# Modulation of the second block: both transfers of a step issued first, then its four one-column products, those of the later transfer leading

## The chip, the cores and the metric

The kernel runs on one core of a Trainium2 chip. A core has a matrix engine (TensorE, PE in the profile), three engines for elementwise work (VectorE, DVE; ScalarE, ACT; GpSimd, POOL), an engine that mostly issues transfers (SyncE, SP) and 16 DMA engines between main memory and the core's on-chip memory. The metric is the device time of one execution in microseconds (us), the median over several runs.

## The reference

Two transformer-like blocks on a sequence of 1024-wide vectors. The first has two layers, each with a pair of recurrent mixers, cross-attention to a memory and a convolutional feed-forward part. The second is conditioned on a vector `c`: six vectors of 1024 numbers each are made from it and shift, scale and gate the block's hybrid mixer (dilated attention beside a gated recurrence) and its mixture of 32 experts.

```python
def second_block(x, c, w_ada, b_ada, ...):
    cond = jax.nn.silu(c)
    mod = cond @ w_ada[l] + b_ada[l]        # 1024 x 6144
    ...                                     # shift, scale, gate of the mixer; shift, scale, gate of the experts
```

The change touches only how `cond @ w_ada` is fed and ordered.

## The kernel before, in words

**The modulation.** `Net.ada` (L1458) computes `mod` as 6144 = 3 x 2048 numbers. Round r of three covers 2048 columns, which stand as four rows of 512 in one bank of the matrix engine's result memory, at partitions 0, 32, 64 and 96. A round has eight steps, k = 0 to 7, one for each 128 of the 1024 input rows. A step brings 128 x 2048 numbers of `w_ada` as two transfers of 128 x 1024 (512 KB each, L1478) into two `raw` tiles, and adds four products to the bank: the stationary operand is one column, `cond[:, k]`, the moving one 128 x 512 of the tile, and the result one row, j = 0 to 3. Rows j = 0, 1 come from the first tile, j = 2, 3 from the second. Each product goes through the helper `mm` (L362), which is why all matrix products of the profile show that line, and each shows as two records. After the last step of a round VectorE adds the bias to the four rows (L1485).

**Where the steps run.** `ada` is a generator. The program calls `fill(point)` at named points of the other work, and a table gives how many steps are drawn there: 18 steps in the RWKV mixer of the first layer (l16, l32, r2, r3, r4), two at xn1 and three at xc1 (around the second layer's cross-attention). The last step is drawn by `drain("a")` at L1695, in the second block's mixer, ahead of `mod_rest` (L1512). `mod_rest` turns the rows into columns (products mc, L1496), makes the gate `gate_m` (products bc, copies L1521) and prepares the router (products rb, `brow` at L265).

**Buffers.** The `raw` tiles come from a pool of five that the modulation shares with the loader of the other weights (`wunit`, L365 on), so a transfer waits on SP until the products that read that buffer are done.

**Order.** The kernel is written with pools and tiles, and a scheduler orders the instructions of each engine when the program is built (L2530). Code that is written in another order can thus shift other instructions too, also far from the place. Names in rows: `mk`, `px`, `pxt`, `py`, `pak`, `pz`, `pm`, `pu` are products of the RWKV mixer; `sc`, `pt`, `po` the score, transpose and output products of the cross-attention (HPT is the copy of pt, L1095); `tm`, `pj` projections, `pa`, `pk`, `pd` the gated recurrence and `as`, `apt`, `pv` the attention of the second block's mixer (HaS its scores, L1720 to L1725, HaPT the copy of apt); `gu`, `dn`, `dx` products of the experts.

Of the kernel before, what the change touches and what calls it, by code (L numbers as in the profile page):

```python
# [225 lines left out]
class Net:  # L226
# [1232 lines left out]
    def ada(self, mrow):  # L1459

        nc = self.nc
        W = self.dr["w_ada_2"][0]
        cond, th = self.cp.tile([128, 8], F32, name="cond"), self.cp.tile([128, 8], F32, name="cth")
        nc.scalar.activation(th, self.V("c"), AF.Tanh, scale=0.5)
        nc.vector.scalar_tensor_tensor(cond, th, 1.0, self.V("c"), op0=OP.add, op1=OP.mult)
        nc.vector.tensor_scalar(cond, cond, 0.5, None, op0=OP.mult)
        for r in range(3):
            nc.sync.dma_start(mrow[r][0:128:32, :], self.dr["b_ada_2"][0, 2048 * r:2048 * r + 2048].rearrange("(j c) -> j c", j=4))
        for u, name in enumerate(("g_post_mix_2", "g_post_ffn_2")):
            nc.sync.dma_start(mrow[3][64 * u:64 * u + 64:32, :], self.dr[name][0].rearrange("(j c) -> j c", j=2))  # L1470
        for r in range(3):
            ps = self.ps("ada")
            for k in range(8):
                for u in range(2):
                    self.n += 1
                    raw = self.rawp.tile([128, 1024], F32, tag="raw", name=f"raw_{self.n}")
                    c0 = 2048 * r + 1024 * u
                    nc.sync.dma_start(raw, W[128 * k:128 * k + 128, c0:c0 + 1024])  # L1478
                    for v in range(2):
                        j = 2 * u + v  # L1480
                        self.mm(ps[32 * j:32 * j + 1, :], cond[:, k:k + 1], raw[:, 512 * v:512 * v + 512], start=(k == 0), stop=(k == 7))
                if k == 7:
                    for j in range(4):
                        row = mrow[r][32 * j:32 * j + 1, :]
                        nc.vector.tensor_tensor(row, ps[32 * j:32 * j + 1, :], row, op=OP.add)  # L1485
                self.nada += 1
                yield 1
# [1046 lines left out]
```

## Time and profile before

| what | us |
|---|---|
| median of 3 runs (2145.54 to 2147.9) | 2145.57 |
| the profiled execution | 2153.04 |
| its span, first to last instruction | 2150.9 |

The trace is of one execution on the chip. PE, DVE, ACT, POOL and SP are the engines; PEld is the load of a stationary operand, which goes on beside products. A row of the timeline gives the start, the duration, the instruction and, in brackets, how long the engine had been idle and what ended that. The granted clock (PEclk) is the share of full speed that TensorE was given. The mean granted clock of the whole span is 0.966.

### The profile page before, as it was taken

Reading aid. Unit: us, or ns where it says so; the run is one execution under the profiler, and the core shown is the slowest. Engines: PE = TensorE matmul, PEld = TensorE weight load, DVE = VectorE, ACT = ScalarE, POOL = GpSimd, SP = SyncE. Lnnn points to the kernel's source line nnn. Section 1 sums busy time; section 2 is a strip of 40 time slices with the busy share of each in tenths; the row PEclk is TensorE's granted clock in tenths of the full one; section 3 lists DMA queues with packets and bytes.
Section 4 is the critical chain, followed back from the end, with each engine's and each line's share of the span. In section 5 each row is a group of like instructions: output and inputs, shape, how many; then the busy total and the mean of one; then the engine's idle time right before and its main releaser. Section 6 shows DMA issues by size and latency. Waiting matters only on the chain.

```text
span 2150.9 us, 37883 instructions
## 1 busy us (share of the span) xinstructions
PE 2015.1 (94%) x15056; PEld 1286.3 (60%) x15056; DVE 937.9 (44%) x1854; ACT 670.9 (31%) x1331; POOL 74.7 (3%) x97
## 2 busy tenths in 40 slices
PE   7999999999997899998989999999999999999997
PEld 6876798999985789997874333333233333333332
DVE  6764655777766457778554111111141111111122
ACT  6523554555654355555333100000000100000011
POOL 1200000000000000002001000000000000000000
PEclk9999999999998899999989999999999999999999
DMA  7459454666634546665858999999899999999992
GB/s 210 147 190 289 126 171 128 192 190 181 184 108 118 166 137 187 182 187 159 310 193 298 376 412 412 412 412 412 359 354 409 409 410 409 410 411 411 407 386 91
DMA packets 327765, 589.14 MB, mean 274 GB/s; under 512 B 25778, under 2 KB 216626, under 8 KB 318242
## 3 DMA queue, kind: packets, MB, share of 16 engines
q1 hardware_dynamic: 327586, 586.70, 76.7%
q8 instruction: 119, 1.95, 0.4%
q14 instruction: 60, 0.49, 0.1%
HBM read 585.58 MB, written 1.05 MB: 273 GB/s over the span
## 4 chain that ended last, share of the span: by engine, by line
PE 87%; DVE 4%; ACT 2%; issue 1%; DMA 1%; POOL 1%; ACTq 0%; SPq 0%; DVEq 0%; POOLq 0%
PE gu L362 22%; PE dn L362 13%; PE ug L362 11%; PE acc L362 9%; PE pj L362 6%; PE mk L362 4%; PE cb L362 3%; PE dx L362 3%; PE qp L362 2%; PE ada L362 1%; PE po L362 1%; PE tm L362 1%; PE accd L362 1%; PE at L2209 1%; DMA raw<-in_w_ada_dram 1%
## 5 line engine op out<-in xcount | busy, mean ns | idle before, releaser
L388 DVE TENSOR_TENSOR lo<-raw,hi 128x512 fp32r<-128x512 f32 x578 | 378.7, 695 | 162.2 <-ACT hi L387 146.8
L387 ACT CAST hi<-raw 128x512 fp32r<-128x512 f32 x578 | 328.7, 618 | 325.4 <-issue 85.0
L362 PE MATMUL gu<-Bring,xg 128*32 128x512 f32 (+1 forms) x3000 | 373.0, 594 | 0.0
L362 PEld LDWEIGHTS gu<-Bring,xg 128*32 128x32 f32 (+1 forms) x3000 | 110.9, 111 | 239.1 <-issue 219.3
L362 PE MATMUL dn<-Bring,ya 128*32 128x512 f32 (+2 forms) x1688 | 231.3, 599 | 1.3
L2317 DVE TENSOR_SCALAR sg<-gu 128x512 f32<-128x512 f32 x32 | 20.6, 686 | 433.1 <-PE gu L362 433.1
L362 PE MATMUL ug<-Bxh,hi 128*128 128x256 f32 x688 | 193.9, 282 | 1.4 <-ACT Bxh L487 1.4
L362 PE MATMUL ug<-Bxl,hi 128*128 128x256 f32 x688 | 193.7, 282 | 0.3 <-DVE Bxl L488 0.3
L362 PE MATMUL ug<-Bxh,lo 128*128 128x256 f32 x688 | 193.6, 282 | 0.0
L2318 ACT ACTIVATE sg<-sg 128x512 f32<-128x512 f32 x32 | 19.7, 629 | 506.6 <-DVE sg L2317 506.6
L362 PE MATMUL gu<-ring,xg 128*32 128x512 f32 (+1 forms) x968 | 174.2, 596 | 0.0
L362 PE MATMUL pj<-Bxh,hi 128*128 128x256 f32 x472 | 140.4, 298 | 8.6 <-ACT hi L387 4.1
L362 PE MATMUL pj<-Bxh,lo 128*128 128x256 f32 x472 | 138.0, 294 | 2.4 <-DVE lo L388 2.4
L362 PE MATMUL pj<-Bxl,hi 128*128 128x256 f32 x472 | 137.4, 292 | 0.9 <-DVE Bxl L488 0.6
L362 PEld LDWEIGHTS dn<-Bring,ya 128*32 128x32 f32 (+1 forms) x1688 | 60.7, 113 | 125.7 <-issue 112.5
L362 PEld LDWEIGHTS ug<-Bxh,hi 128*128 128x128 f32 x688 | 129.8, 189 | 3.9 <-ACT Bxh L487 1.8
L362 PEld LDWEIGHTS ug<-Bxl,hi 128*128 128x128 f32 x688 | 130.2, 189 | 1.9 <-DVE Bxl L488 0.5
L362 PEld LDWEIGHTS ug<-Bxh,lo 128*128 128x128 f32 x688 | 130.1, 189 | 0.0
L362 PEld LDWEIGHTS pj<-Bxh,hi 128*128 128x128 f32 x472 | 93.0, 197 | 13.5 <-ACT hi L387 5.3
L362 PEld LDWEIGHTS pj<-Bxh,lo 128*128 128x128 f32 x472 | 92.5, 196 | 5.2 <-DVE lo L388 3.0
L362 PEld LDWEIGHTS pj<-Bxl,hi 128*128 128x128 f32 x472 | 92.9, 197 | 3.8 <-issue 1.8
L362 PEld LDWEIGHTS gu<-ring,xg 128*32 128x32 f32 (+1 forms) x968 | 47.3, 111 | 75.9 <-issue 73.4
(725 smaller groups left out, 3141.5 us busy)
## 6 DMA issues: line engine op xcount, KB each, us to landing
Bring<-in_w_gu_dram SPq DMA_DIRECT2D x366, 512.0 KB, 10.2
Bring<-in_w_down_dram SPq DMA_DIRECT2D x198, 512.0 KB, 10.8
ring<-in_w_gu_dram SPq DMA_DIRECT2D x73, 1024.0 KB, 12.5
raw<-in_ffn_w_up_dram SPq DMA_DIRECT2D x84, 512.0 KB, 4.2
ring<-in_w_down_dram SPq DMA_DIRECT2D x29, 1024.0 KB, 13.3
raw<-in_w_ada_dram SPq DMA_DIRECT2D x48, 512.0 KB, 5.0
raw<-in_ffn_w_down_dram SPq DMA_DIRECT2D x42, 512.0 KB, 3.6
raw<-in_xattn_wkv_dram SPq DMA_DIRECT2D x32, 512.0 KB, 4.0
```

Of the source, the lines that this page charges most:

```text
L362: return self.nc.tensor.matmul(out, lhsT, rhs, start=start, stop=stop, skip_group_check=True)
L387: nc.scalar.copy(hi[:, s], raw[:, s])
L388: nc.vector.tensor_tensor(lo[:, s], raw[:, s], hi[:, s].bitcast(F32), op=OP.subtract)
L2209: nc.tensor.transpose(pt[:, f, :], act[:, 128 * f:128 * f + 128], self.ident)
L2317: nc.vector.tensor_scalar(g, pglu, 7.0, None, op0=OP.min)
L2318: nc.scalar.activation(g, g, AF.Silu, scale=1.702)
```

## The change

In `ada` a step now asks for both tiles and issues both transfers first, and then runs its four products in the order j = 2, 3, 0, 1, so that the two fed by the second transfer come first.

```diff
             for k in range(8):
+                raws = []
                 for u in range(2):
                     self.n += 1
                     raw = self.rawp.tile([128, 1024], F32, tag="raw", name=f"raw_{self.n}")
                     c0 = 2048 * r + 1024 * u
                     nc.sync.dma_start(raw, W[128 * k:128 * k + 128, c0:c0 + 1024])
-                    for v in range(2):
-                        j = 2 * u + v
-                        self.mm(ps[32 * j:32 * j + 1, :], cond[:, k:k + 1], raw[:, 512 * v:512 * v + 512], start=(k == 0), stop=(k == 7))
+                    raws.append(raw)
+
+                for j in (2, 3, 0, 1):
+                    self.mm(ps[32 * j:32 * j + 1, :], cond[:, k:k + 1], raws[j // 2][:, 512 * (j % 2):512 * (j % 2) + 512], start=(k == 0), stop=(k == 7))
                 if k == 7:
```

On TensorE, at the three steps drawn at xc1 in the cross-attention of the second layer (`ada_2117` is the bank, `raw_...` the tile a pair of products reads; lines with - are of the kernel before, with + of the changed one):

```order
 L362 MATMUL sc_7816<-BkT_221,Bq_7529 128x256 x4
+L362 MATMUL ada_2117<-raw_7919,cond 1x512 x2
 L362 MATMUL ada_2117<-raw_7917,cond 1x512 x2
-L362 MATMUL ada_2117<-raw_7921,cond 1x512 x2
+L362 MATMUL ada_2117<-raw_7927,cond 1x512 x2
 L362 MATMUL ada_2117<-raw_7925,cond 1x512 x2
-L362 MATMUL ada_2117<-raw_7929,cond 1x512 x2
+L1093 MATMUL pt_7831<-c_70,BP_7799 128x128
+L362 MATMUL ada_2117<-raw_7935,cond 1x512 x2
 L362 MATMUL ada_2117<-raw_7933,cond 1x512 x2
-L1093 MATMUL pt_7831<-c_70,BP_7799 128x128
 L1093 MATMUL pt_7831<-c_70,BP_7800 128x128
```

The second tile of each step (7919, 7927, 7935 now; 7921, 7929, 7937 before) leads, and the last step stands as a group of four behind the first transpose pt. Before, five pairs ran ahead of the four transposes and one behind them.

On TensorE, at the end of the last step, in the second block's mixer: before, both pairs stand further up among the tm products, and behind the last pk there comes

```order
L1667 MATMUL pk_10750<-c_70,Bkd_10517 128x128
L1496 MATMUL mc_10910<-c_70,Bmrow_225 128x128 x4
L1496 MATMUL mc_10916<-c_70,Bmrow_226 128x128 x4
L362 MATMUL bc_10923<-Bmrow_225,c_70 128x512
L362 MATMUL bc_10926<-Bmrow_225,c_70 128x512
L362 MATMUL pd_10765<-Hvx_10763,Hkt_10752 128x512
L362 MATMUL rb_10934<-wr,modc 1x32 x8
```

and in the changed kernel, at the same place,

```order
L1669 MATMUL pk_10750<-c_70,Bkd_10517 128x128
L362 MATMUL ada_2117<-raw_10895,cond 1x512
L1498 MATMUL mc_10910<-c_70,Bmrow_225 128x128 x4
L362 MATMUL pd_10765<-Hvx_10763,Hkt_10752 128x512
L362 MATMUL pd_10773<-Hvx_10771,Hkt_10752 128x512
L362 MATMUL pd_10781<-Hvx_10779,Hkt_10752 128x512
L362 MATMUL pd_10789<-Hvx_10787,Hkt_10752 128x512
L1498 MATMUL mc_10916<-c_70,Bmrow_226 128x128 x4
L362 MATMUL bc_10923<-Bmrow_225,c_70 128x512
L362 MATMUL bc_10926<-Bmrow_225,c_70 128x512
L362 MATMUL rb_10934<-wr,modc 1x32 x8
```

The last product of the modulation has moved behind the last pk; the transposes mc of row block 226 and what follows them stand behind four pd products instead of ahead of them.

On TensorE, in the attention of the same mixer, behind the last of the tm products (one piece of the difference):

```order
 L362 MATMUL tm_11216<-lo_11280,Bxh_10312 128x512
-L362 MATMUL as_11333<-Bka_10949,Bqa_10948 128x128 x2
-L362 MATMUL as_11357<-Bka_10949,Bqa_10948 128x256
-L1729 MATMUL apt_11322<-c_70,HaS_11316 128x128 x4
-L362 MATMUL as_11357<-Bka_10949,Bqa_10948 128x256
+L362 MATMUL as_11313<-Bka_10949,Bqa_10948 128x256 x2
+L362 MATMUL as_11333<-Bka_10949,Bqa_10948 128x128 x4
+L362 MATMUL as_11357<-Bka_10949,Bqa_10948 128x256 x2
 L362 MATMUL as_11377<-Bka_10949,Bqa_10948 128x256 x2
 L362 MATMUL as_11397<-Bka_10949,Bqa_10948 128x128 x4
+L1731 MATMUL apt_11322<-c_70,HaS_11316 128x128 x4
```

The first score products (as_11313 and half of as_11333) stood 24 tm products earlier; they now stand behind the last of them, a few products ahead of the transposes apt_11322 that read their result.

## Rows read from the trace of the kernel before

**Rows 1.** The page: chain that ended last, shares by engine.
```profile
PE 87%; DVE 4%; ACT 2%; issue 1%; DMA 1%; POOL 1%; ACTq 0%; SPq 0%; DVEq 0%; POOLq 0%
```
**Rows 2.** Windows: length, busy (instructions) of each engine, PEclk, DMA share, GB/s.
```profile
150.00:200.00 50.00, 48.97 (x738) 26.68 (x734) 17.81 (x34) 9.12 (x17) 0.64 (x2) 1.00 0.94 304
1000.00:1050.00 50.00, 50.00 (x347) 37.54 (x346) 38.52 (x78) 18.82 (x33) 11.76 (x10) 1.00 0.93 309
1300.00:1500.00 200.00, 181.85 (x1542) 64.86 (x1538) 35.48 (x79) 16.90 (x34) 0.00 (x0) 0.97 1.02 412
```
**Rows 3.** Tile ada: count, min/median/max ns, first and last start, shape.
```profile
L362 PE MATMUL ada<-raw,cond x192: 590/591/593, 127.3 to 1006.4; 128*1 128x512 f32 x192
```
**Rows 4.** Lines, 126 to 196 us: count, busy us, mean ns, idle before.
```profile
L362 PE MATMUL ada<-raw,cond 128*1 128x512 f32 x144 | 31.4, 591 | 0.7 <-DMA raw<-in_w_ada_dram 0.7
```
**Rows 5.** Timeline of PE: start us, us, instruction, count, idle before.
```profile
133.90 1.03 PE L362 MATMUL ada<-raw,cond 128*1 128x512 f32 x4
...
153.67 1.04 PE L362 MATMUL ada<-raw,cond 128*1 128x512 f32 x8
...
158.96 1.03 PE L362 MATMUL ada<-raw,cond 128*1 128x512 f32 x4 [0.42 <-DMA raw<-in_w_ada_dram]
160.22 1.03 PE L362 MATMUL ada<-raw,cond 128*1 128x512 f32 x4 [0.23 <-DMA raw<-in_w_ada_dram]
...
193.73 1.03 PE L362 MATMUL ada<-raw,cond 128*1 128x512 f32 x4
...
690.22 1.90 PE L362 MATMUL ada<-raw,cond 128*1 128x512 f32 x16
```
**Rows 6.** Waits of SP, 118 to 200 us: total us, times, longest.
```profile
SPq L1478 <- PE ada L362: 39.1, 22, 6.1
```
**Rows 7.** Tile raw, 120 to 200 us: transfers.
```profile
DMA to landing us min/median/max: 3.6/6.0/7.6
```
**Rows 8.** Timeline of PE at xc1.
```profile
732.38 1.03 PE L362 MATMUL ada<-raw,cond 128*1 128x512 f32 x4 [1.51 <-DMA raw<-in_w_ada_dram]
733.33 1.99 PE L362 MATMUL po<-HPT,Bmv 128*128 128x256 f32 x8
```
**Rows 9.** Timeline of DVE at xc1.
```profile
730.90 0.69 DVE L1095 COPY HPT<-pt 128x512 f32<-128x512 f32 x1 [0.38 <-PE pt L1093]
```
**Rows 10.** Timeline of PE at the last step.
```profile
1005.96 1.03 PE L362 MATMUL ada<-raw,cond 128*1 128x512 f32 x4
...
1019.46 2.84 PE L362 MATMUL pd<-Hvx,Hkt 128*128 128x512 f32 x6
```
**Rows 11.** Timeline of DVE there.
```profile
1008.90 2.78 DVE L1485 TENSOR_TENSOR Bmrow<-ada,Bmrow 1x512 f32<-1x512 f32 x4
...
1013.04 0.69 DVE L1518 TENSOR_TENSOR Bmrow<-Bmrow 64x512 f32<-64x512 f32 x1
...
1018.81 1.28 DVE L1521 COPY gate_m<-bc 128x512 f32<-128x512 f32 x2
...
1020.58 0.17 DVE L265 TENSOR_TENSOR brow<-rb,brow 1x32 f32<-1x32 f32 x1
```
**Rows 12.** Timeline of PE in the second mixer's attention.
```profile
1062.01 1.57 PE L362 MATMUL as<-Bka,Bqa 64*128 64x256 f32 x8
...
1075.99 1.97 PE L362 MATMUL pv<-Bva,HaPT 128*128 128x64 f32 x8 [0.78 <-DVE HaPT L1731]
```
**Rows 13.** Timeline of ACT: last exponential of the first scores.
```profile
1066.06 0.19 ACT L1725 ACTIVATION_READ_ACCUMULATOR HaS<-HaS,amx 128x1 f32 x1
```
**Rows 14.** Timeline of PE, later in the attention.
```profile
1095.41 1.63 PE L1729 MATMUL apt<-c,HaS 128*128 128x128 f32 x4 [1.20 <-ACT HaS L1725]
```
**Rows 15.** Windows in the attention, columns as in rows 2.
```profile
1070.00:1075.00 5.00, 4.94 (x36) 3.82 (x34) 3.05 (x5) 2.49 (x10) 0.00 (x0) 1.00 0.70 255
1075.00:1080.00 5.00, 4.22 (x20) 4.03 (x20) 1.97 (x3) 1.09 (x4) 0.00 (x0) 0.60 0.00 0
```
**Rows 16.** Timeline of PE in the expert stage.
```profile
1560.60 0.49 PE L362 MATMUL dx<-sl,h 128*128 128x128 f32 x2
```

## The prediction

> **What bounds the kernel now.** I read the page's chain of waits first: the chain that ended last runs through TensorE (PE) for 87% of the span, through a DMA for 1% [rows 1]. That is a mean over two regimes, so I took busy time by windows [rows 2]. Where the modulation's products stand, PE is busy for 48.97 and 50.00 of 50 us; from 1300 us on the transfer of expert weights runs at 412 GB/s with the DMA engines at a share of 1.02, and it is DMA that sets the end. The expert stage starts when PE has finished what lies ahead of it, so a shift of PE before 1150 us passes one to one to the end, and I count PE time.
>
> The modulation's own products cost little in all: 192 records of 591 ns, two for a product, so 96 products in 24 steps of four, from 127.3 to 1006.4 us [rows 3]. Of the 24 steps 18 stand between 126 and 196 us, where these records cover 31.4 us of PE time [rows 4]. The rest are two at 690, three at 727 and one at 1004 us.
>
> How a product is priced comes from the timeline [rows 5]. A lone pair of products (four records, 133.90) takes 1.03 us. A group of four whose two tiles lie ready (eight records, 153.67) takes 1.04.  So products for different column groups run beside each other, and a step costs 1.0 us if it is issued as four together and 2.0 if as two lone pairs. Seventeen groups in the stretch are lone pairs, from 133.90 to 193.73. At 690.22 eight products with all tiles ready take 1.90, so 0.95 a step.
>
> The same stretch has a second limit. At 158.96 and 160.22 PE waits for a tile, 0.42 and 0.23 us, and starts as it lands [rows 5]: one tile per 1.26 us then. SyncE (SP), which issues the transfers, waits 39.1 us in 22 waits for the modulation's products to free one of five buffers [rows 6], and a transfer takes 3.6 us at the least and 6.0 in the middle from issue to landing [rows 7].
>
> **The change part by part.**
>
> (1) The 18 steps between 127 and 195 us. On SP the order of issue hardly moves, since each transfer still waits for its buffer; the products move. Without any waiting, 18 steps of 0.95 would cost 17.1 us in place of 31.4. The order built for the new kernel splits three steps between other work, which makes 21 rounds or 20.0 us, so 11.4 us less. Against that, the first tile of each pair is now held until the second has landed and its two products have run, 1.26 us or more, so that a later transfer starts that much later. I carried the steps forward: a product starts when PE is free and its tile is there; a tile lands 3.65 us after its issue or 1.28 after the tile before it (near the 3.6 and the 1.26 of the rows); its issue waits for the last product on that buffer. On the order of before this puts the end at 195.2 us, against 194.7 in the trace (last pair at 193.73 plus 0.96). On the new order it gives 194.3: PE gains 1.8 us up to 153, spends it waiting for a tile landing near 156.7, and then loses between 0.5 and 2.2 us at each of seven further tiles, 11.3 us of waits in all where before, by the same reckoning, has 4.9. The difference is -0.8 us; with the irregular part of the landings shuffled it runs from -3 to +2.
>
> The Trainium skill, "TensorEngine Tiling (Array Packing)", section "Tiling Modes", says that column tiles work independently and in parallel. The 1.04 us for four products agrees. By that rule alone this term would be -11.4, the first rival below.
>
> (2) The two steps at 690.22: all tiles there before and after, 0.
>
> (3) The three steps at 727.24. Before, five pairs run, then four transposes pt, then PE waits 1.51 us for the last tile, runs the last pair and starts po at 733.33 [rows 8]. The copy HPT (0.69 us), which po needs, runs from 730.90 to 731.59, inside that wait [rows 9]. In the new order the last step, both pairs, stands behind the first transpose and three transposes behind it. The tile's issue waits for the same buffer, so it lands as before, at about 732.3; then four products 0.95, three transposes 0.6, HPT 0.69 and 0.3 for the two hand-overs: po starts near 734.9. That is +1.5; nothing on PE covers it. Bounds: 0.3 (if the tile lands 1.2 earlier) to 2.
>
> (4) The last step. Before, two lone pairs stand in the tm products, the second at 1005.96 [rows 10], and VectorE adds the bias from 1008.90, 2.78 us, 6 us ahead of the transposes mc that read the row [rows 11]. In the new order one record pair of the first tile comes after the pa and pk products: three groups in place of two, +1.05. The four adds and the gain (2.78 + 0.69 = 3.47 us) then start near 1018 rather than at 1008.90. The four pd products moved in between (eight records; six take 2.84 us, so 3.8 [rows 10]) cover them; behind them the two copies gate_m (1.28), which stood at 1018.81, and the state updates stand ahead of brow (0.17 at 1020.58), for which the second rb product and with it pj wait: about 1.2 us that nothing covers. Sum +2.3, bounds +0.5 and +4. PE is busy for all of 1000 to 1050 [rows 2], so neither side has slack.
>
> (5) The attention after it. The score products as at 1062.01 stood between tm products, and the tm products behind them, some 6 us, hid their softmax [rows 12, 13]. In the new order they come behind the last tm product, and the transposes apt follow them after 3 us: the chain of add, maximum and exponentials that they wait for ended at 1066.24, 4.2 us after the start of as, so about 1.2 us are bare, and the pv and apt behind wait 1.0 and 0.8 more, +3.0. Against it, in the new order the exponentials for the apt at 1095.41 stand earlier in ScalarE's queue, which should end its wait of 1.20 us and a little of the next [rows 14]: -1.5. I take +1.5, bounds -1 and +4.
>
> (6) In the expert stage one pair of dx records (0.49 us at 1560.60) moves out from among the dn products on which the stream of weights waits [rows 16]: -0.4, bounds -0.5 and 0.
>
> Sum: -0.8 + 0 + 1.5 + 2.3 + 1.5 - 0.4 = +4.1 us. Against the profiled execution (2153.04 us: span 2150.9 and 2.1 around it) that is 2157.1. The median of the runs, 2145.57, lies 7.5 us under that execution; I put the same difference on it: 2149.7, and take 2149.3 because the two largest terms are those with the widest bounds towards zero.
>
> **The rivals.**
>
> Side by side pays in full. For it: 1.03 against 1.04 us for two and four products. Against it: PE starts products at the moment of landing at 158.96 and 160.22, and the five buffers, not PE, decide when a tile is asked for [rows 6]; holding a pair together makes each stay longer. If landings kept up the sum is -11.4 + 4.9 = -6.5: 2139 us.
>
> Nothing changes. The SP queue issues two transfers in a row before and after, so the first half of the change would do nothing, and the waits of terms (3) to (5) would fall into waits that stand there anyway, as the 1.51 at 732 and the 1.20 at 1095 do. Result -1 to +1: 2145.6. Against it: at 1004 to 1070 PE shows no idle time into which they could fall.
>
> The clock. At 1075.99 PE has waited 0.78 us between short apt and pv products [rows 12], and in 1075 to 1080 its granted clock is 0.60 of full, between its levels of 1.2 and 2.4 GHz [rows 15]: of 4.22 us of busy time 40% or 1.7 us would not have been needed at full clock. If the bare waits of term (5) bring the fall on at 1070, the as, apt and pv products there, some 6 us of PE work, run at half speed as well (+3), and with the waits of (3) and (4) at their upper bounds (+0.5 and +1.7) the sum becomes 4.1 + 3 + 2.2 = +9.3: 2154.9. It decides from the point where apt waits over 1 us. Against it: the clock stays at 1.00 in 150 to 200 in spite of waits for tiles [rows 2].
>
> The Trainium skill, "TensorE: Matmul & The Clock Gate", section "HAM oscillation", says that short groups of products with waits for data between them let the clock fall to half again and again; here 150 to 200 us shows no such fall and 1075 shows one.
>
> **How the numbers follow.** A measurement of this kernel can tell about 0.2%, 4.3 us, from no change: faster is under 2141.3, slower over 2149.9. The forecast, a loss of 1 to 7 us, has 0.46, a little under half of it beyond 2149.9; nothing changes 0.24; side by side in full 0.14, and some of its way 0.02; the clock 0.14. So faster 0.16, same 0.44, slower 0.40 (0.21 from the forecast, 0.14 from the clock, 0.05 from several upper bounds together). The range must reach towards both rivals: 2140.5 to 2155. The forecast's own range is 2146.5 to 2152.5.
>
> **What would show it.** In the new profile the ada records between 126 and 196 us should cover some 23 to 26 us, in groups of eight, with PE's waits for raw tiles at about 11 us there, and the first product after the last of them should start within 2 us of 194.7. po after the steps at 727 should start about 1.5 us later than now relative to them; rb's second product should wait for brow about 1 us; apt near 1072 should wait over 1 us for ScalarE. The prediction is wrong if the stretch to 195 us ends over 4 us sooner (landings kept up), or if terms (3) to (5) together cost under 1 us or over 8.

## The result, and the profile after

The changed kernel is slower: 2167.32 us median of 7 runs (2158.39 to 2170.35) against 2151.28 for the kernel before (7 runs, 2145.54 to 2153.49), ratio 1.0075 with a 95% interval of 1.0054 to 1.0096. The forecast had 2149.3 and a range to 2155.0. It was a loss of 3.7 us, and 16.0 were measured: the sign was right and the size four times too small. The forecast also started from 2145.57, the median of the three runs known then; over seven runs the kernel before stands at 2151.28, so 5.7 of the 18.0 us between forecast and result are of the starting point and 12.3 of the change.

The page's chain and three windows of the changed kernel (columns as in [rows 2]) come first:

```profile
PE 86%; DVE 5%; ACT 2%; DMA 2%; issue 1%; POOL 1%; ACTq 0%; DVEq 0%; POOLq 0%
```
```profile
150.00:200.00 50.00, 41.65 (x642) 24.24 (x636) 11.74 (x23) 6.67 (x13) 0.53 (x1) 0.83 0.87 279
1000.00:1050.00 50.00, 47.76 (x291) 35.73 (x289) 39.32 (x76) 21.60 (x35) 9.38 (x8) 0.97 0.80 264
1300.00:1500.00 200.00, 181.97 (x1545) 64.53 (x1538) 34.32 (x75) 15.78 (x32) 0.00 (x0) 0.97 1.02 412
```

The expert stage is what it was. In 150 to 200 PE is busy for 7.3 us less than in [rows 2], the granted clock is 0.83 in place of 1.00, and in 1000 to 1050 idle time has appeared.

To find where the 13.0 us between the two spans (2150.9 and 2163.9) arise I matched instructions: the n-th product of a name in one trace with the n-th of that name in the other, and took by how much it starts later. The table gives how that lag changes in a stretch (us of the trace before at its ends), as medians over the products within 1 us of an end. Row 1 is the changed kernel; the other rows are the experiments below.

| kernel | 0-111 | 111-223 (18 steps) | 223-716 | 716-800 (xc1) | 800-1000 | 1000-1135 (last step, attention) | 1135-2055 (experts) |
|---|---|---|---|---|---|---|---|
| changed | -1.2 | **+4.1** | -0.2 | **+6.5** | 0.0 | **+3.8** | +0.1 |
| e1 issue first | -1.9 | +0.7 | -0.3 | 0.0 | 0.0 | -0.5 | -6.1 |
| e2 RWKV only | -2.6 | +2.9 | +1.3 | +0.1 | 0.0 | -0.1 | 0.0 |
| e3 xc1 only | -1.7 | -0.9 | +1.4 | +6.6 | 0.0 | +6.6 | -0.3 |
| e4 last only | +2.0 | +1.4 | +2.5 | -3.4 | +0.6 | -1.2 | -10.3 |
| e4 again | +0.4 | +1.3 | -0.8 | -0.2 | 0.0 | +3.2 | -4.9 |
| l1 xc1 old | +0.6 | +5.6 | +1.0 | +0.1 | 0.0 | +2.7 | -12.8 |
| c1 xc1 busy | 0.0 | +4.1 | -0.8 | +3.1 | 0.0 | +3.5 | -1.7 |
| p1 last ahead | -0.8 | +7.3 | 0.0 | +6.4 | 0.0 | +0.6 | -0.1 |
| c3 RWKV busy | +0.2 | +9.9 | +4.1 | +3.0 | +0.6 | +8.8 | -6.5 |
| b1 first six | -1.8 | +1.5 | +2.0 | +0.1 | +0.6 | +7.4 | +2.0 |
| h5 before, six buffers | +3.7 | +1.7 | +8.8 | -0.8 | +2.6 | -3.2 | +0.3 |
| h6 after, six buffers | +5.9 | +6.7 | +1.7 | +2.0 | +1.3 | -1.2 | +3.7 |

e1 has the same order of instructions on PE as the kernel before, so its row shows how far two traces of one program differ: up to 2 us in a stretch, 6 us in the experts' stage. A single trace can stray further: e4's first one gains 3.4 us at xc1 with the old form there. Over the 18 steps the old form gave -0.9 to +1.4 (e1, e3, e4 twice), the new form in all 18 steps +2.9 to +7.3 (c3, with products added, +9.9).

**The 18 steps.** Line group of the ada products from 126 to 200 us, and PE's timeline there, after:

```profile
L362 PE MATMUL ada<-raw,cond 128*1 128x512 f32 x144 | 25.0, 701 | 7.9 <-DMA raw<-in_w_ada_dram 7.9
```
```profile
154.60 1.04 PE L362 MATMUL ada<-raw,cond 128*1 128x512 f32 x8 [1.62 <-DMA raw<-in_w_ada_dram]
157.80 1.89 PE L362 MATMUL ada<-raw,cond 128*1 128x512 f32 x8 [2.15 <-DMA raw<-in_w_ada_dram]
...
177.19 1.46 PE L362 MATMUL ada<-raw,cond 128*1 128x512 f32 x8 [4.12 <-DMA raw<-in_w_ada_dram]
180.05 1.89 PE L362 MATMUL ada<-raw,cond 128*1 128x512 f32 x8
183.82 1.89 PE L362 MATMUL ada<-raw,cond 128*1 128x512 f32 x8
189.18 1.89 PE L362 MATMUL ada<-raw,cond 128*1 128x512 f32 x8
193.03 1.04 PE L362 MATMUL ada<-raw,cond 128*1 128x512 f32 x8
```
The granted clock there, after (columns as in [rows 2]):
```profile
170.00:175.00 5.00, 3.07 (x66) 1.86 (x60) 0.85 (x2) 0.00 (x0) 0.00 (x0) 1.00 0.77 228
175.00:180.00 5.00, 2.81 (x30) 1.47 (x30) 0.00 (x0) 0.00 (x0) 0.00 (x0) 0.77 0.83 302
180.00:185.00 5.00, 5.00 (x50) 2.05 (x48) 0.00 (x0) 0.75 (x2) 0.00 (x0) 0.50 0.92 304
185.00:190.00 5.00, 4.54 (x59) 2.87 (x56) 1.70 (x7) 0.37 (x1) 0.00 (x0) 0.50 0.87 292
```
The products do run side by side: the busy time falls from 31.4 us [rows 4] to 25.0, and a step that finds its data takes 1.04. By 178 us (before's time) PE is 5.4 us ahead by the matched starts, 1.2 of them from before 111. It gets there early only to wait 4.12 us for one tile, and behind that wait the clock is 0.50, 1.2 GHz: a step takes 1.89 in place of 1.04 and all products around it slow down alike. By 187 PE is 3.9 us behind, a turn of 9.2 us: 4.1 of waiting, most of the rest at half clock. Behind the two shorter waits, 1.62 and 2.15, the clock was down as well, at 0.72 between 155 and 160, and the step at 157.80 takes 1.89 too.

The tile of the long wait is no later than it was. It is the second one of the thirteenth step, the 26th transfer of the modulation; its issue, before (first two rows: issue, and PE starting on it) and after:

```profile
170.37 1.28 SPq L1478 DMA_DIRECT2D raw<-in_w_ada_dram  x1
177.11 1.03 PE L362 MATMUL ada<-raw,cond 128*1 128x512 f32 x4
```
```profile
169.36 1.54 SPq L1479 DMA_DIRECT2D raw<-in_w_ada_dram  x1
```
It was issued by 171.65 and PE started on it at 177.11, after 0.06 us of waiting; now it is issued by 170.90 and PE starts on it, as it lands, at 177.19. The tile of the wait of 2.15 us is the one that PE waited 0.42 us for at 158.96 [rows 5]; it lands at 157.80, 1.2 us sooner, which is the lag at 111. PE comes earlier and these tiles do not. Behind the long wait the products free their buffers later, and the transfers start later too.

An estimate of the whole stretch: without the slow clock the ada products would cover some 21 us, 10 less than before; PE waits 7.2 us more for tiles; and the busy time in windows of 5 us from 155 to 195, each times what its granted clock lacks of 1.00, gives some 7 us. That makes about +4, as measured.

**xc1.** PE's timeline after:
```profile
735.01 1.89 PE L362 MATMUL ada<-raw,cond 128*1 128x512 f32 x8 [2.97 <-DMA raw<-in_w_ada_dram]
...
738.51 3.78 PE L362 MATMUL po<-HPT,Bmv 128*128 128x256 f32 x8 [0.79 <-DVE HPT L1095]
742.09 1.06 PE L1093 MATMUL pt<-c,BP 128*128 128x128 f32 x4
744.02 3.75 PE L362 MATMUL po<-HPT,Bmv 128*128 128x256 f32 x8 [0.88 <-ACT hi L387]
```
```profile
735.00:740.00 5.00, 4.21 (x15) 1.83 (x16) 2.23 (x4) 2.27 (x4) 0.00 (x0) 0.50 0.98 359
```
The tile lands when it did (735.01 less the 2.6 us by which this trace lags at 716 is 732.4). PE comes to it sooner, with two groups of four products and one transpose ahead of it in place of five pairs and four transposes, so the wait of 1.51 us [rows 8] has become 2.97; and po behind it takes 3.78 us where it took 1.99.

**The last step.** PE, VectorE and GpSimd after:
```profile
1025.05 1.02 PE L362 MATMUL ada<-raw,cond 128*1 128x512 f32 x2
...
1032.33 0.66 PE L1498 MATMUL mc<-c,Bmrow 128*128 128x128 f32 x4 [2.24 <-DVE Bmrow L1520]
...
1037.42 0.59 PE L362 MATMUL rb<-brow,c 1*128 1x32 f32 x2
```
```profile
1027.35 2.78 DVE L1487 TENSOR_TENSOR Bmrow<-ada,Bmrow 1x512 f32<-1x512 f32 x4
...
1030.76 1.52 DVE L1520 TENSOR_TENSOR Bmrow<-Bmrow 64x512 f32<-64x512 f32 x1
```
```profile
1023.79 9.38 POOL L1675 TENSOR_TENSOR Hvx<-Bvr,Bct 128x512 f32<-128x512 f32 x8 [33.48 <-ACT Bvr L1624]
```
The adds start 1.3 us after the last product has ended, when VectorE is done with two lo and HaT. They take 2.78 us as in [rows 11], but the gain (L1520) takes 1.52 us in place of 0.69 while GpSimd works on Hvx, and mc waits 2.24 us for it. The pa and pk products behind run at half clock again in part (granted clock 0.72 from 1035 to 1040). rb, which I expected to wait for brow, has its input by then.

### The profile page after: what moved, and what is told of

It reads as the page before. It is cut to its first block, busy times and chain, and to the rows that moved or that the text cites. A ratio compares the mean times of both kernels' runs of the same rounds, so it can differ in the third digit from the quotient of the medians.

```text
span 2163.9 us, 37884 instructions
## 1 busy us (share of the span) xinstructions
PE 2015.9 (93%) x15056; PEld 1289.3 (60%) x15056; DVE 937.6 (43%) x1854; ACT 671.6 (31%) x1331; POOL 74.6 (3%) x97
## 3 DMA queue, kind: packets, MB, share of 16 engines
HBM read 585.58 MB, written 1.05 MB: 271 GB/s over the span
## 4 chain that ended last, share of the span: by engine, by line
PE 86%; DVE 5%; ACT 2%; DMA 2%; issue 1%; POOL 1%; ACTq 0%; DVEq 0%; POOLq 0%
PE gu L362 22%; PE dn L362 13%; PE ug L362 11%; PE acc L362 9%; PE pj L362 6%; PE mk L362 4%; PE cb L362 3%; PE dx L362 3%; PE qp L362 2%; PE po L362 1%; PE ada L362 1%; PE accd L362 1%; PE tm L362 1%; DVE lo L388 1%; DMA raw<-in_w_ada_dram 1%
```

## The experiments

In e2, e3, e4, l1 and b1 the two forms stand side by side and a set of step numbers (0 to 23) chooses. In p1, which has all 24 steps in the set, PE's order up to 1000 us is that of the changed kernel.

```diff
+                    if self.nada not in NEW:
+                        for j in (2 * u, 2 * u + 1):
+                            product(j, raw)
+                if self.nada in NEW:
+                    for j in (2, 3, 0, 1):
+                        product(j, raws[j // 2])
```

**e1, transfers first, products in the old order.**
```diff
-                for j in (2, 3, 0, 1):
+                for j in (0, 1, 2, 3):
```


> Both transfers of a step are issued first, the products stay in the order 0, 1, 2, 3. Theory (the order of the products does it all): TensorE's and SP's order come out as in the kernel before, so the time is that of before within 0.2%, and the groups of ada products between 126 and 196 us again cover about 31 us. Rival (the issue of both transfers ahead holds the buffers longer): most of the loss stays, at least +8 us.

Measured: ratio 0.9991 (0.9979 to 1.0004), and the order on PE is that of before. So are those on SP, VectorE and ScalarE. Issuing both transfers first does nothing; the order of the products is the whole change. The kernel before had a median of 2152.98 beside it.

**e2, steps 0 to 17** (`NEW = range(0, 18)`).

> The changed form in the 18 steps of the RWKV mixer only, the form of before in the other six. Theory: the trace loses about 4 us between 126 and 205 us (PE waits for tiles some 8 us or more and the clock falls to half behind the longest wait) and nothing behind it; total +2 to +6 us. Rival (the stretch is hidden, the loss is made by what the scheduler moved in the second block): 0 to +1 us.

Measured: 1.0018 (1.0003 to 1.0034), +2.9 us in the stretch, one wait of 3.47 us at 175 and steps of 1.89 behind it, and the order of before from 716 us on. As the theory has it.

**e3, steps 20 to 22** (`NEW = range(20, 23)`).

> The changed form in the three steps at xc1 only. Theory: +5 to +7 us between 725 and 800 us, of which +2.5 to the first po and the rest because the products behind the wait run at half clock; what the scheduler moves at the last step comes with it and adds up to +5 there. Rival (the clock fell only by chance in the one trace): +1.5 us at xc1, as forecast.

Measured: 1.0058 (1.0041 to 1.0075), +6.6 at xc1, and +6.6 between 1000 and 1135 though the last step's code is the old one: with xc1 in the new form the scheduler places that step elsewhere. e2 and e3 together, 1.0018 and 1.0058, make up the 1.0075 of the change.

**e4, step 23**, twice (`NEW = (23,)`).

> The changed form in the last step only. Theory: here the scheduler leaves both pairs together among the tm products, one group of four in place of two lone pairs, so -1 us at 1003 to 1007 and nothing else before the experts; total -1 to 0 us. Rival (the order 2, 3, 0, 1 itself costs in the last step): +4 us between 1000 and 1050, as in the changed kernel.

> The changed form in the last step only, a second time with more rounds: -0.1 to -0.3% if the first result (0.9979) holds; within 0.1% if that was scatter.

Measured: 0.9979 (0.9964 to 0.9993) and 0.9975 (0.9961 to 0.9989). Both pairs stay together among the tm products, as forecast, but that saves nothing in 1000 to 1135 (-1.2 and +3.2). Of the gain, some 5 us lie between 1920 and 1960 us, where the scheduler has put dx products ahead of dn; l1 has the same there. So it is the fastest kernel of these, but not by the modulation.

**l1, all but xc1** (`NEW = (*range(20), 23)`).

> The changed form everywhere but in the three steps at xc1. In the order built for it the last step and what follows stand as in the kernel before, but with one group of four. Theory (xc1 makes its own loss and, through the scheduler, that of the last step): +3 to +5 us between 111 and 223, 0 at xc1, -1 to +1 between 1000 and 1135; total within 0.3% of before. Rival (the last step's own change makes the loss there): +4 to +5 us between 1000 and 1050, total +0.35% or more.

Measured: 0.9993 (0.9975 to 1.0011); +5.6, +0.1 and +2.7 in the three places, and the gain among the experts as in e4. With xc1 in the old form the last step stands in the old order again. The total holds, but by luck: the 18 steps still lose, and that the sum is 0 is owed to the experts' stage.

**c1, PE kept busy in the wait at xc1**: products into a spare bank ahead of the third step (`DUM = {22: 22}`).
```diff
+                if self.nada in DUM:
+                    last = next(i for i in reversed(nc.cur_bb.bb.instructions) if i.engine == mybir.EngineType.PE)
+                    one, wm = self.ident.bitcast(BF16), self.ps("wm")
+                    with self.tc.issue_after(last):
+                        for _ in range(DUM[self.nada]):
+                            self.mm(wm[:, 0:256], one[:, 0:128], one)
```


> The changed kernel, with 22 products that nobody reads (128x256, some 0.11 us each) put between the products of the second and the third step at xc1, where PE waits 2.97 us for the last tile. The output is unchanged. Theory (most of the loss at xc1 is the clock that falls behind that wait): PE waits under 1 us there, the granted clock stays at 1.00 in 735 to 745, the two po groups take 2.0 us each in place of 3.8, and the loss between 716 and 800 us falls from +6.5 to +2 to +3. Rival (the loss is the later start of po and its chain of copies): it stays at +6 or more.

PE's timeline of c1:
```profile
732.42 2.03 PE L366 MATMUL wm<-c 128*128 128x256 bf16 x17
...
735.84 1.04 PE L366 MATMUL ada<-raw,cond 128*1 128x512 f32 x8 [0.73 <-DMA raw<-in_w_ada_dram]
736.81 0.55 PE L1097 MATMUL pt<-c,BP 128*128 128x128 f32 x3
739.75 1.99 PE L366 MATMUL po<-HPT,Bmv 128*128 128x256 f32 x8 [2.39 <-DVE HPT L1099]
...
743.05 1.97 PE L366 MATMUL po<-HPT,Bmv 128*128 128x256 f32 x8 [0.87 <-DVE HPT L1099]
```
The wait falls to 0.73, the granted clock is 1.00 from 730 to 750, po takes 1.99 and 1.97, and the stretch loses +3.1, just over the +2 to +3 of the theory. So 3.4 us less, but that is not all that the clock was worth, since c1 has a delay of its own. Its VectorE runs two lo ahead of the copy HPT, and PE waits 2.39 us for HPT; in the changed kernel HPT comes first, as the last pt ends, and PE waits 0.79. VectorE in c1, then in the changed kernel:
```profile
737.80 1.29 DVE L392 TENSOR_TENSOR lo<-raw,hi 128x512 fp32r<-128x512 f32 x2 [3.92 <-ACT hi L391]
739.01 0.68 DVE L1099 COPY HPT<-pt 128x512 f32<-128x512 f32 x1
```
```profile
737.77 0.69 DVE L1095 COPY HPT<-pt 128x512 f32<-128x512 f32 x1 [4.61 <-PE pt L1093]
```
Without that delay, 1.6 us, c1 would lose some 1.5 (an estimate), and the clock would be worth some 5. The slow rows of the changed kernel say the same: 1.89 for 1.04, 0.90 for 0.55, 3.78 for 1.99, 1.06 for 0.60 and 3.75 for 1.96 are 5.2 us. The time, 1.0080 (1.0062 to 1.0097), doesn't show a gain: its median of 2167.88 rests on four runs that spread over 9 us, and the reading stands on the trace alone.

**p1, the last step at a higher priority** (`with self.tc.high_priority(offset=400)` around the products of step 23).

> The changed kernel, with the four products of the last step given a higher priority, so that they stand as one group ahead among the tm products and mc, bc and rb stand as in the kernel before. Theory (the loss between 1000 and 1050 us is made by the last product, the adds and the transposes behind it standing late): the +4.9 there becomes -1 to 0. Rival (the tile is late or the moved recurrence products cost it): +3 or more stays.

VectorE's and PE's timelines of p1:
```profile
1026.77 5.75 DVE L392 TENSOR_TENSOR lo<-raw,hi 128x512 fp32r<-128x512 f32 x4
```
```profile
1033.38 0.63 PE L366 MATMUL rb<-wr,modc 128*1 128x32 f32 x16 [2.54 <-DVE modc L1517]
```
Measured: 1.0038 (1.0015 to 1.0060), about half of the loss. The old order is back, but 3.2 us remain at 1049 (2.6 are given back in the attention), so the -1 to 0 of the theory is missed: rb waits 2.54 for VectorE, whose four lo take 5.75 us beside GpSimd's Hvx; in the kernel before the same four took 4.19, and two of them elsewhere 1.29. The Trainium skill, "SBUF — State Buffer", section "SBUF: two separate sides", says that a VectorE instruction with both inputs in that on-chip memory and a GpSimd instruction that reads it lock each other out of a shared pair of ports. The slower lo and the gain of 1.52 us agree, and so do the adds, with one input in the result memory, which take 2.78 us either way; no run here removes GpSimd.

**h5 and h6, six raw buffers** before and after (`("rawp", 6)`, `BLKB = 23`).

> The kernel before with six raw buffers in place of five (and one block buffer less, to make room). It is the base for the next run. Both theories: within 0.5% of before; the stretch from 126 to 200 us up to 3 us shorter, since PE waits for tiles there and SP for buffers.

> The changed kernel with six raw buffers in place of five (and one block buffer less). Theory (holding a pair until its later tile has landed makes the next transfer late): with a sixth buffer the long wait near 177 us falls under 1.5 us, the clock stays at 1.00 to 195 us, and against the kernel before with six buffers this stretch is 3 to 8 us shorter, the sum of both xc1 and this stretch no longer a loss. Rival (the transfers themselves are the limit, whatever the buffers): the wait stays over 3 us, the clock falls, and the stretch is again about 3 to 4 us longer than with the products in their old order.

PE's timeline of h6:
```profile
187.55 1.34 PE L362 MATMUL ada<-raw,cond 128*1 128x512 f32 x8 [3.10 <-DMA raw<-in_w_ada_dram]
...
190.78 1.89 PE L362 MATMUL ada<-raw,cond 128*1 128x512 f32 x8
```
Measured: 1.0081 (1.0060 to 1.0101) and 1.0086 (1.0062 to 1.0111); the six-buffer kernel costs more than expected. The scheduler orders it differently from the start, so the lost block buffer isn't shown to be what costs, and the two are compared with each other. Over the 18 steps h6 loses 6.7 us and h5 1.7, so the new form still costs 5.0 with a sixth buffer, with a wait of 3.10 and half clock behind it. My theory that the held buffer alone makes the wait falls. At xc1 neither kernel waits for a tile any more; there h5 gains 0.8 and h6 loses 2.0.

**c3, PE kept busy before the long wait** (as c1, `DUM = {12: 40}`).

> The changed kernel, with 40 products that nobody reads (128x256, some 0.11 us each, 4.5 us) ahead of the thirteenth step in the RWKV mixer, the one that PE waits 4.12 us for at 177 us. The output is unchanged; the scheduler puts them some products earlier than the wait stood, so a part of the wait can be left. Theory (half of the loss of this stretch is the clock behind that wait): PE waits under 1.5 us there, the granted clock stays at 0.95 or more in 175 to 195, the later groups of eight records take 1.04 us and not 1.89, and the loss between 111 and 223 us falls from +4.1 to between -1 and +1.5. Rival (landings alone decide, the slow groups sit in time that PE would wait anyway): +3 to +6.

PE's timeline of c3, among the 18 steps and at xc1:
```profile
175.01 4.54 PE L366 MATMUL wm<-c 128*128 128x256 bf16 x40
179.48 1.04 PE L366 MATMUL ada<-raw,cond 128*1 128x512 f32 x8
...
185.16 1.75 PE L366 MATMUL ada<-raw,cond 128*1 128x512 f32 x8 [2.03 <-DMA raw<-in_w_ada_dram]
188.98 1.89 PE L366 MATMUL ada<-raw,cond 128*1 128x512 f32 x8
...
746.82 1.04 PE L366 MATMUL ada<-raw,cond 128*1 128x512 f32 x8 [3.19 <-DMA raw<-in_w_ada_dram]
...
749.12 3.38 PE L366 MATMUL po<-HPT,Bmv 128*128 128x256 f32 x8 [0.78 <-DVE HPT L1099]
...
753.82 1.96 PE L366 MATMUL po<-HPT,Bmv 128*128 128x256 f32 x8 [0.88 <-DVE HPT L1099]
```
Measured: 1.0105 (1.0077 to 1.0133), +9.9 in the stretch: a miss. The wait at the thirteenth step is gone, but later tiles, whose transfers wait for the delayed products, come later too; PE waits 2.03 at 185 and the clock falls after all. Filling the wait was not free here. At xc1 the same trace gives a control: nothing was changed there, the wait is 3.19, but the clock fell later and rose sooner, and the loss is +3.0 and not +6.5. There po starts 1.6 us late by the lag at 716, and the first po at 3.38 in place of 1.99 makes the rest.

**b1, steps 0 to 5 and 23** (`NEW = (*range(6), 23)`).

> The changed form in the first six steps of the RWKV mixer (up to 153 us, where the groups of four put PE ahead) and in the last step, the old form elsewhere; the scheduler moves a few hundred other products later on, so the stretch to 223 us is what is read. Theory (landings, and the buffers that set them, bound the stretch, so a lead of PE is given back at the next tile): PE is 2 to 3 us ahead at 150 us, waits for tiles by 158 us, has no wait over 2 us after that, the clock stays at 1.00 to 195 us, and between 111 and 223 us the change is -1 to +1.5. Rival (the lead is kept where no later step holds a pair): -2.5 or more.

PE's timeline and two windows of b1:
```profile
158.02 1.03 PE L364 MATMUL ada<-raw,cond 128*1 128x512 f32 x4 [1.30 <-DMA raw<-in_w_ada_dram]
...
177.46 1.03 PE L364 MATMUL ada<-raw,cond 128*1 128x512 f32 x4 [1.36 <-DMA raw<-in_w_ada_dram]
```
```profile
175.00:180.00 5.00, 3.64 (x50) 1.51 (x46) 0.00 (x0) 0.37 (x1) 0.00 (x0) 1.00 0.96 369
180.00:185.00 5.00, 5.00 (x82) 2.41 (x80) 0.71 (x4) 0.74 (x2) 0.00 (x0) 1.00 0.96 336
```
Measured: PE 2.4 us further ahead at 152 than at 111, as the theory has it, back to 0.4 at 161, no wait over 1.36, clock 1.00, +1.5 in the stretch. The lead of PE is given back at the next tiles, and with waits of 1.36 us at the most the clock holds in this stretch. The total is 1.0044 (1.0027 to 1.0061), of which +7.4 come from the last step's place again.

## Why the prediction was wrong, point by point

What failed is the step "I carried the steps forward", in term (1), and with it terms (3) and (4): it let PE run at full clock behind every wait, and put the fall of the clock at nothing. The runs show it to cost some 7 us of PE time among the 18 steps, some 5 at xc1 and 1 to 2 at the last step, all estimates from rows.

Term (1), -0.8, measured +4.1. The lead was 2.9 us at 152 (the term had 1.8) and was lost in waits as forecast. I had 11.3 us of waits in eight places; the trace has 7.9 us of idle PE before products, in three, and behind them the clock fell to 0.72 and 0.50. The term's own figures don't close either: 11.4 us less of products and 6.4 more of waits (11.3 against 4.9) make -5.0, while the ends of the two reckonings gave -0.8. The rival by which side by side pays in full fell with the same rows: the price of 1.04 us a step held, but the tiles landed when they did before.

Term (2), 0: held, -0.2 from 223 to 716.

Term (3), +1.5, measured +6.5. The order and the late po were right, in size too: po starts 1.6 us late in c3, and c1 would lose some 1.5 without the delay on VectorE. What the term left out is the half clock behind the wait, the other 5 us: 3.78, 1.06 and 3.75 for po, pt and po in place of 1.99, 0.60 and 1.96. A share of that is chance from trace to trace, as c3 shows with +3.0.

Term (4), +2.3, measured +4.9 to 1049 us, a size outside its bounds: I charged brow, and the wait was 2.24 us at mc. The adds began where I had put them (1027.35 less the lag of 9.2 us at 1000 is 1018.2), but the gain took 1.52 us and not 0.69 beside GpSimd, copies of the recurrence stood between, and some of the products behind ran at half clock.

Term (5), +1.5, measured -1.1 (4.9 to 3.8): wrong sign, just past its lower bound of -1. The bare wait for the first apt was 0.36 us and not 1.2:
```profile
1085.47 0.93 PE L1731 MATMUL apt<-c,HaS 128*128 128x128 f32 x4 [0.36 <-ACT HaS L1727]
```
Term (6), -0.4, measured +0.1 over the whole expert stage, less than two traces of one program differ there.

Terms (3) to (5) cost 10.3 us in the trace, over the 8 that I had named as a sign of being wrong. The 25.0 us of ada records in groups of eight came as I had said.

The third rival had the right mechanism in the wrong place. I looked for a fall of the clock where [rows 15] showed one and took 150 to 200 as safe because it stood at 1.00 before [rows 2]; but before, PE's waits there were 0.42 and 0.23 us, and it was the change that turned them into 1.62 to 4.12. The rival's 2154.9 us thus counted the clock in the attention alone. The Trainium skill, "TensorE: Matmul & The Clock Gate", section "HAM oscillation", which I cited for the attention, describes this: products thinner than the wait for their data, and a clock that falls at the wait. The granted clocks of 0.50 behind 4.12 and 2.97 us agree.

What stays open: what sets the landings among the 18 steps, which hardly moved when PE came earlier. Five buffers alone don't explain it (h6); transfers that wait for delayed products (c3) are part of it; no run here separates them from the transfer's own time. Open too is the clock's share of the 18 steps as an experiment: c3 was to remove it and did not, so there it is read from the granted clock alone.

## What to carry to other kernels

Work that gets cheaper on an engine in front of a supply that does not come sooner only gathers its waits in fewer places. Here these cost more than the shorter ones of before, because what stood behind them on TensorE ran at half clock. When a change lengthens a wait on TensorE, price what stands behind it at 1.2 GHz too (some 10 us behind the 4.12 and the 2.97), also where the trace before shows full clock throughout. Short waits are not safe either: at xc1 of the kernel before, the third po ran at half clock behind waits of 1.31, 1.30 and 0.78 us, and in e4's first trace, behind the same waits, it did not (1.99 us), which makes half of the 3.4 us there. Before, then e4:
```profile
743.36 0.33 PE L1093 MATMUL pt<-c,BP 128*128 128x128 f32 x1 [1.31 <-DVE BP L1117]
744.99 0.90 PE L1093 MATMUL pt<-c,BP 128*128 128x128 f32 x3 [1.30 <-DVE BP L1117]
746.68 3.78 PE L362 MATMUL po<-HPT,Bmv 128*128 128x256 f32 x8 [0.78 <-DVE HPT L1095]
```
```profile
752.51 1.99 PE L364 MATMUL po<-HPT,Bmv 128*128 128x256 f32 x8 [0.78 <-DVE HPT L1097]
```
And where a scheduler orders the program, a small edit can move a step far from it: compare the whole order, and undo the edit place by place.

## What the runs showed of the hardware that I had not expected

Four one-column products on different column groups take 1.04 us at full clock and 1.89 at half, two take 1.03. VectorE's lo (128x512, some 0.64 us each) takes 1.05 to 1.44 us while GpSimd multiplies tiles. And one program, with the same order, differs by 6 us in the expert stage between two traces (e1 against before).
